# New cost figures in a planned kernel, the memory transposed by the host, the filters' network first, a bias read backwards

## The chip, the cores and the metric

The kernel runs on one core of a Trainium2 chip. The metric is device time in microseconds (us), the median over runs. Engines are named as in the profile: PE (TensorE, the matrix products; PEld its weight loads), DVE (VectorE), ACT (ScalarE), POOL (GpSimd), SP (SyncE, which issues nearly all DMAs).

## The reference, cut to what matters

Two layers act on 256 tokens of width 1024, with a second input `mem` of 256 rows.

- Layer 0: `h = rmsnorm(x)`; `z = h @ hy_w_in` (1024 x 2048). Three of its four blocks of 512 channels go through a short convolution and a gated long convolution (Hyena, order 2). The long filters come from a small network: `h = sin(fr * (feats @ w1 + b1))`, `h = sin(fr * (h @ w2 + b2))`, `h @ w3`, times a decay, divided by the sum of magnitudes, then a transform. The fourth block is the query of a cross attention over `m = rmsnorm(mem)`, with `kv = m @ w_kv`. Both halves go through `w_out`, then a SwiGLU feed-forward with hidden width 2816.
- Layer 1: `z = h @ at_w_in` (1024 x 5120): dilated attention with 3 groups x 4 heads of width 128 and a bias from a table of relative positions, `s = q k / sqrt(128) + bias`, softmax, and the groups combined; again cross attention over `mem`, `w_out`; then a mixture of 8 experts, of which each token takes 2: `(silu(x @ wg[e]) * (x @ wu[e])) @ wd[e]`.

All in float32. The weights of the eight experts alone are 277 MB.

## The kernel before, in words

**Arithmetic.** A float32 factor is split in two parts of type float32r, `hi` (ACT, a rounding copy) and `lo` (DVE, the rest): `split`. A product is three matmuls, hi·hi, hi·lo, lo·hi (`mm3`). Weights come from memory in units of 1 MB (128 x 2048 floats, `load`, kind "stream"); each unit becomes two pairs of 128 x 1024 by one CAST on ACT and one subtraction on DVE each (`weights`, kind "split"), and feeds 12 matmuls of 512 columns (or 24 of 256). Small products of the filters' network are plain float32; each appears in the profile as two MATMUL records. Transposes go through PE with the identity `kt[:, :128]` (`tr`).

**Planner.** Nothing is issued as it is written. Every call (`nc.vector...`, `nc.tensor...`) is recorded by `Plan.add` with a modelled length from `Plan.cost`. `order` then simulates the five queues: `backwards` gives each operation a time by which it has to run (`late`), and going forward each engine takes, of what is ready and finds room, the one with the smallest `late`. Buffers (24 slots of 128 x 2048 floats, 8 PSUM banks) are given out in that simulated order. The result is one fixed order for each engine; on the chip semaphores alone decide the times. A modelled load is bytes / 360e3 us one after the other, and SP does not run more than `BACKLOG` = 6 us ahead of it; a matmul of n float32r columns is max(0.107, 0.0025 + n x 0.4167e-3) us. Kind "dense" marks the weight products, which keep their written order; kind "first" gives an operation a base time 50 us early.

**Stages.** Layer 0's start (`run`, `layer0_mix`): constants `kt`, `sm`; `x` and its norm (`norm_T`), 16 transposes and splits to `hT`; the filters' network (`taps`: product, a chain of vector operations to bring the argument into the range of Sin, Sin, twice), `filters`, `spectrum`; then `memory(0, True)`: `mem` is loaded by rows, squares are summed for its norm (`self.mr`, used later as a scale of the keys), and its rows are transposed (`rows_T`, 16 transposes) and split with the gain to `mT`; first dense block `kv`. Then the Hyena blocks, cross attention, feed-forward, `memory(1, True)` (again loads and transposes `mem`), layer 1, the experts (`moe_layer`, `expert`: per expert 33 units, 396 matmuls of 512 columns), each ending with an indirect DMA that adds its rows to the output (`add_rows`).

**Bias.** `bias_of` reads the bias of a head as a sliding window from a scratch in DRAM, which gives the rows in reversed order. `head` splits it and adds it on PE: two matmuls of 512 columns with the exchange matrix `flip` begin each of the 8 accumulations of scores (4 heads, 2 halves), and softmax reads the scores from PSUM.

Of the kernel before, what the change touches and what calls it, by code (L numbers as in the profile page):

```python
# [13 lines left out]
F32R = mybir.dt.float32r  # L14
# [3 lines left out]
OP = mybir.AluOpType  # L18
# [4 lines left out]
S = 256  # L23
# [5 lines left out]
NB = 32  # L29
NUNIT = 33  # L30


# [3 lines left out]
C_GX, C_GM, C_GK = 58, 82, 90  # L36
N_SM = 106


K_ID, K_FLIP, K_TRI, K_ONE, K_IOTA, K_I8, K_FOLD, K_ROW = 0, 128, 256, 384, 512, 640, 648, 656  # L40
N_K = 660

# [77 lines left out]
class _Eng:  # L120
# [3 lines left out]
    def __getattr__(self, fn):  # L124
# [4 lines left out]
       ("scalar", "vector"): 0.13, ("vector", "scalar"): 0.17, ("scalar", "tensor"): 0.27, ("vector", "tensor"): 0.25}  # L129
FREE = 0.2  # L130
TABLES = {AF.Exp, AF.Silu, AF.Sin}
LOAD = 1.3
# [3 lines left out]
class Plan:  # L136
# [17 lines left out]
    def reset(self):  # L154
        self.ops, self.pe_time = [], 0.0
        for m in self.fixed:
            m.left, m.log, m.end = 0, [], 0.0
        taken = [m.where.i for m in self.fixed if m.kind == "sb"]
        self.whole = [i for i in range(N_SLOT) if i not in taken][::-1]
        self.free = {(dt, k): [] for dt in (F32, F32R) for k in (512, 1024)}  # L160
        self.free_tiny = list(range(N_TINY))[::-1]
        self.free_bank = list(range(8))[::-1]
# [156 lines left out]
    def cost(self, eng, fn, a, kw, aps):  # L319

        n = max((self.width(x) for x in aps), default=1)
        if fn == "add_rows":
            return ISSUE
        if fn == "dma_start":
            ap = aps[0]
            return self.width(ap) * ap.ap[0][1] * 4 / 360e3
        if eng == "tensor":
            if fn == "transpose":
                return 0.109
            r = kw["rhs"]  # L330
            n = self.width(r.on(r.t.ref))
            if kw["rhs_dt"] == F32R:
                return max(0.107, 0.0025 + n * 0.4167e-3)
            return 4 * max(0.054, 0.0025 + n * 0.4167e-3)
        if eng == "scalar":
            ptr = isinstance(kw.get("scale"), View) + isinstance(kw.get("bias"), View)
            return 0.05 + 0.834e-3 * n + 0.2 * ("accum_out" in kw) + 0.09 * ptr
        if eng == "vector":
            return 0.07 + (6.4e-3 if fn == "reciprocal" else 1.04e-3) * n + 0.06 * (fn == "scalar_tensor_tensor")
        if kw.get("op") == OP.pow:  # L340
            return 0.35 + 0.16 * n
        return 0.05 + 2.3e-3 * n if fn == "tensor_tensor" else 0.05 + 3.5e-3 * n if fn == "tensor_copy" else 0.05

    def add(self, eng, fn, a, kw):
        kind, after = kw.pop("kind", None), kw.pop("after", ())
        op = Op()
# [6 lines left out]
        for v in every:  # L353
            w = any(v is o for o in outs)
            lo, hi, p0, p1, ap = self.region(v)
# [8 lines left out]
            for e in m.log:  # L364
                l, h, q0, q1, ew, j = e
# [7 lines left out]
        if fn == "matmul":  # L373
            r = kw["rhs"]
# [20 lines left out]
    def order(self):  # L395
# [35 lines left out]
        while done < len(ops):  # L431
# [9 lines left out]
            while queue and queue[0].start is not None:  # L441
                queue.pop(0)
            self.frontier = queue[0].late
            while self.coming and self.coming[0][2].base is not None:
# [75 lines left out]
    def backwards(self):  # L520
# [45 lines left out]
        for op in ops:  # L566
            op.late = op.rev

# [50 lines left out]
class _Kernel:  # L619
# [229 lines left out]
    def run(self):  # L849
# [16 lines left out]
        self.ident = kt[:, K_ID:K_ID + 128]  # L866
        self.flip = plan.at([128, 128], "flip", F32R)
        nc.scalar.copy(out=self.flip, in_=kt[:, K_FLIP:K_FLIP + 128])
        self.tri = kt[:, K_TRI:K_TRI + 128]
# [8 lines left out]

        nc.scalar.activation(self.tiny(8), self.mhalf, AF.Sin, kind="first")
        xt = plan.x  # L880
        self.x = [xt[:, a * D:(a + 1) * D] for a in range(2)]
# [177 lines left out]
    def layer0_mix(self):  # L1059
        nc, io = self.nc, self.io  # L1060
        hT, dft = self.pair(2048), self.pair(512)
        h8 = hT.rearrange("p (k t) -> p k t", k=8)
        by_parity = lambda t: t.rearrange("p (k t) -> p k t", k=2)
        self.norm_T(self.x, self.scaled(hT, C_GX, natural=True))
        taps = self.taps()
        w3 = self.load(io["w3"], 1024)
# [7 lines left out]
        self.filters(*taps, w3, decay, skip, by_parity(raw))  # L1074
        kT = self.memory(0, True)

# [45 lines left out]
    def memory(self, l, keys):  # L1122

        if keys:
            rows = self.tokens(self.io["mem"])
            if not l:
                self.mr = [self.rms(t) for t in rows]
            self.mT = self.pair(2048)
            self.rows_T(rows, self.scaled(self.mT, C_GK + 8 * l))
        ps = self.dense_block(self.lhs(self.mT))  # L1130
        t = self.pair(1024)
        (self.heads_T if keys else self.rows_of)(ps, t, rms=self.mr)
        return t
# [91 lines left out]
    def head(self, h, at, vecs, out):  # L1225

        nc = self.nc
        hk = self.pair(1024)
        self.split(hk, self.bias_of(vecs, h))
        hk = hk.rearrange("p (a n) -> p a n", a=2)  # L1230
        q, k, v = ([at[f"{n}{g}", h] for g in range(3)] for n in "qkv")
        half = lambda p, a: p[:, a * 128:(a + 1) * 128]
        pT = self.pair(1024).rearrange("p (s a t) -> p s a t", s=4, a=2)
        for a in range(2):
            ps = self.bank()
            nc.tensor.matmul(ps, lhsT=self.flip, rhs=hk.hi[:, a], start=True, stop=False)
            nc.tensor.matmul(ps, lhsT=self.flip, rhs=hk.lo[:, a], start=False, stop=False)
            self.mm3(ps[:, :256], half(q[0], a), k[0], False, False)
            for g in (1, 2):
                self.mm3(ps[:, 128 + 128 * g:256 + 128 * g], half(q[g], a), half(k[g], a), False, g == 2)  # L1240
            sc = self.slot(512)
            g1 = lambda t: t.rearrange("p (z k) -> p z k", z=1)
            self.softmax_rows(g1(ps), 1, g1(sc))
            tp = self.bank()
            for s in range(4):
                self.tr(tp[:, s * 128:(s + 1) * 128], sc[:, s * 128:(s + 1) * 128])
            self.split(pT[:, :, a], tp.rearrange("p (s t) -> p s t", s=4))
        po = self.bank()
        for s in range(2):
            self.mm3(po[:, :256], half(v[0], s), pT[:, s].rearrange("p a t -> p (a t)"), s == 0, False)  # L1250
        for s in (2, 3):
            for a in range(2):
                self.mm3(po[:, a * 128:(a + 1) * 128], half(v[s - 1], a), pT[:, s, a], False, s == 3 and a == 1)
        self.split(out[:, h], po[:, :256])
# [248 lines left out]
def _constants():  # L1503
    c = {}
    k = np.zeros((128, N_K), np.float32)
    k[:, K_ID:K_ID + 128] = np.eye(128)
    k[:, K_FLIP:K_FLIP + 128] = np.eye(128)[::-1]
    k[:, K_TRI:K_TRI + 128] = np.triu(np.ones((128, 128)), 1)
# [27 lines left out]
    oh = np.zeros((33, 5, 256), np.float32)  # L1536
    r = np.arange(255) - 127
    for kind in range(5):
# [41 lines left out]
def _inputs(v):  # L1580
# [21 lines left out]
    io["x"] = v["x"][0]  # L1602
    io["mem"] = v["mem"][0]
    io["rel_bias"] = v["rel_bias"]
    fw = np.zeros((64, 448), np.float32)
# [28 lines left out]
```

## Time and profile before

| what | value |
|---|---|
| median of 3 runs | 1332.57 us (1332.44 to 1333.93) |
| profiled execution, its own time | 1331.97 us |
| its span, first to last instruction | 1330.1 us |
| PE busy / DVE busy / ACT busy | 1307.0 / 1077.9 / 895.7 us |
| memory moved | 372.84 MB, mean 280 GB/s |
| mean granted clock of TensorE | 0.998 |

PE's matmuls overlap: the length of one record (397 ns for 512 columns) is longer than the step from one to the next, so a row "x85, 19.55 us" has 84 steps and one length. Nearly all instructions are issued by one line of the planner (L299), so groups are told apart by their tiles: `b` is a PSUM bank, `s` a slot, `tiny` a small buffer, `kt` the constants.

### The profile page before, as it was taken

To read this page: it belongs to the slowest core of one execution; us is meant where nothing else is said; L and a number is where in the kernel's file an instruction comes from. 1 tells how busy PE (TensorE), PEld (TensorE's weight loads), DVE (VectorE), ACT (ScalarE), POOL (GpSimd) and SP (SyncE) were. 2 spreads that over 40 slices of the span, in tenths; PEclk is the share of its full clock that TensorE was granted. 3 is DMA by queue.
4 is the path that set the end of the run, shared out by engine and by line. 5 is a ranking of instruction groups with operands and counts; after the bars stand their busy time and mean duration, and the time that the engine had idled before them with its cause. 6 is when DMAs were issued, how large, how long until landed. Compare 5 with 4: busy or idle time off the path is not lost.

```text
span 1330.1 us, 16843 instructions
## 1 busy us (share of the span) xinstructions
PE 1307.0 (98%) x6256; PEld 1073.6 (81%) x6256; DVE 1077.9 (81%) x1429; ACT 895.7 (67%) x1190; POOL 41.3 (3%) x38
## 2 busy tenths in 40 slices
PE   6999999999999999999999999999999999999997
PEld 4798888888878888888888888888888778777775
DVE  7989775554578777898999989999988888988886
ACT  7455754444566566687877777876876777777774
POOL 0100000000001000000000000000000000000000
PEclk9999999999999999999999999999999999999999
DMA  9548533357435456299999999999999999999992
GB/s 370 222 146 293 212 138 129 134 187 271 173 127 207 126 172 248 97 371 354 341 375 348 342 367 356 356 375 360 336 365 368 364 351 345 376 360 351 368 354 77
DMA packets 57437, 372.84 MB, mean 280 GB/s; under 512 B 6415, under 2 KB 10595, under 8 KB 13700
## 3 DMA queue, kind: packets, MB, share of 16 engines
q1 hardware_dynamic: 56196, 367.49, 73.8%
q0 software_dynamic: 1152, 4.19, 1.7%
q8 instruction: 51, 0.84, 0.2%
q14 instruction: 38, 0.31, 0.1%
HBM read 365.88 MB, written 5.79 MB: 279 GB/s over the span
## 4 chain that ended last, share of the span: by engine, by line
PE 88%; issue 7%; ACT 2%; DMA 1%; DVE 1%; SPq 0%; POOL 0%; POOLq 0%; ACTq 0%; DVEq 0%
PE b L299 88%; ACT s L299 2%; DVE s L299 1%; DMA out<-s,tiny 1%; DMA sm<-sm 0%; SPq L299 0%; POOL out L296 0%; POOLq L1375 0%; DVE tiny L299 0%; ACTq L299 0%; DVE cg L299 0%; POOLq L296 0%; DVEq L299 0%
## 5 line engine op out<-in xcount | busy, mean ns | idle before, releaser
L299 PE MATMUL b<-s,s 128*128 128x512 f32 (+1 forms) x5674 | 1279.0, 383 | 2.9 <-DVE s L299 0.9
L299 PEld LDWEIGHTS b<-s,s 128*128 128x128 f32 x5674 | 1003.9, 188 | 215.3 <-DVE s L299 15.0
L299 DVE TENSOR_TENSOR s<-s,s 128x1024 fp32r<-128x1024 f32 (+3 forms) x729 | 832.7, 1187 | 124.5 <-ACT s L299 123.6
L299 ACT CAST s<-s 128x1024 fp32r<-128x1024 f32 (+1 forms) x705 | 689.8, 1039 | 128.6 <-PE b L299 96.6
L299 DVE TENSOR_TENSOR s<-b,s 128x512 f32<-128x512 f32 (+5 forms) x206 | 123.0, 609 | 63.4 <-ACT s L299 58.9
L299 ACT CAST s<-b 128x512 fp32r<-128x512 f32 (+3 forms) x118 | 58.3, 504 | 130.5 <-PE b L299 127.4
L299 ACT ACTIVATE s<-b 128x512 f32<-128x512 f32 (+3 forms) x81 | 42.9, 539 | 68.7 <-PE b L299 68.6
L299 PE MATMUL b<-kt,s 128*128 128x128 f32 (+1 forms) x480 | 88.1, 273 | 1.2 <-DVE s L299 1.0
L299 PEld LDWEIGHTS b<-kt,s 128*128 128x128 f32 x480 | 65.1, 146 | 18.6 <-ACT s L299 2.2
L299 ACT ACTIVATE s<-b,tiny 128x512 f32<-128x512 f32 (+2 forms) x58 | 34.0, 611 | 28.0 <-PE b L299 20.7
L299 DVE SCALAR_TENSOR_TENSOR s<-b,sm,s 128x256 fp32r<-128x256 f32 (+1 forms) x88 | 38.0, 478 | 8.2 <-ACT s L299 6.6
L299 ACT ACTIVATE s<-b,sm 128x256 fp32r<-128x256 f32 (+1 forms) x84 | 35.2, 487 | 11.9 <-PE b L299 11.4
L296 POOL DMA_INDIRECT out<-s,tiny x8 | 14.4, 1794 | 761.3 <-ACT s L299 569.5
L299 POOL TENSOR_TENSOR tiny<-tiny,mhalf 128x1 f32<-128x1 f32 (+4 forms) x23 | 26.5, 1152 | 341.5 <-DVE tiny L299 327.1
L299 ACT ACTIVATE s<-x 128x512 f32<-128x512 f32 x16 | 10.1, 631 | 17.7 <-DVE x L299 13.5
L299 PE MATMUL b<-s 128*128 128x512 f32 (+4 forms) x40 | 11.9, 389 | 10.0 <-DMA s<-fw 5.9
L299 DVE TENSOR_TENSOR tiny<-tiny 128x1 f32<-128x1 f32 (+4 forms) x81 | 12.2, 156 | 10.2 <-ACT s L299 8.3
L299 DVE TENSOR_REDUCE tiny<-b 128x2 f32<-128x512 f32 (+3 forms) x25 | 12.3, 495 | 9.5 <-PE b L299 9.4
L299 DVE TENSOR_REDUCE tiny<-s 128x4 f32<-128x512 f32 (+3 forms) x26 | 13.9, 558 | 5.3 <-ACT s L299 5.3
L299 PEld LDWEIGHTS b<-s 128*128 128x128 f32 (+2 forms) x40 | 6.7, 195 | 11.6 <-DMA s<-fw 5.9
L299 DVE TENSOR_TENSOR x<-b,x 128x512 f32<-128x512 f32 x12 | 8.3, 691 | 9.1 <-PE b L299 9.0
L299 ACT COPY s<-b 128x512 f32<-128x512 f32 x11 | 6.3, 584 | 13.6 <-PE b L299 13.4
(65 smaller groups left out, 157.4 us busy)
## 6 DMA issues: line engine op xcount, KB each, us to landing
s<-w_moe SPq DMA_DIRECT2D x264, 1024.0 KB, 7.1
s<-w_ffn SPq DMA_DIRECT2D x33, 1024.0 KB, 4.9
s<-w_at SPq DMA_DIRECT2D x20, 1024.0 KB, 5.1
s<-w_kv SPq DMA_DIRECT2D x8, 1024.0 KB, 7.9
s<-w_hy SPq DMA_DIRECT2D x8, 1024.0 KB, 16.3
s<-w_out SPq DMA_DIRECT2D x8, 1024.0 KB, 4.9
s<-mem SPq DMA_DIRECT2D x4, 512.0 KB
out<-x SPq DMA_DIRECT2D x3, 512.0 KB
```

The lines of the kernel that those rows point to most:

```text
L296: self.nc.gpsimd.indirect_dma_start(out=out, out_offset=bass.IndirectOffsetOnAxis(ap=index, axis=0), in_=rows, in_offset=None, compute_op= ...
L299: getattr(getattr(self.nc, op.eng), op.fn)(*args, **kw)
```

## The change

1. Planner: loads at 390e3 instead of 360e3 bytes per us; float32r matmuls at max(0.11, 0.0137 + n x 0.4167e-3).
2. 14 products of zeros (128 x 128, float32) at the very start, kind "warm", which get `late` = -60; kind "first" for all of `taps()`, which is now called before anything else of the layer.
3. `mem` is also passed in transposed by the host (`mem_t`); `mT` is split from it directly. Layer 0 still loads `mem` by rows for its norm, layer 1 doesn't. `memory(0, True)` is called before the norm of `x`.
4. The table of the bias is written in reverse order; DVE adds the bias to the scores, reading it with a step of -1, into a slot; softmax reads that slot. `flip` and its 16 matmuls, and the split of the bias, are gone.

```diff
+WARM = 14
+RATE = 390e3
-            return self.width(ap) * ap.ap[0][1] * 4 / 360e3
+            return self.width(ap) * ap.ap[0][1] * 4 / RATE
-                return max(0.107, 0.0025 + n * 0.4167e-3)
+                return max(0.11, 0.0137 + n * 0.4167e-3)
-        kind, after = kw.pop("kind", None), kw.pop("after", ())
+        kind, after = kw.pop("kind", self.kind), kw.pop("after", ())
-            self.frontier = queue[0].late
+            self.frontier = max(0.0, queue[0].late)
-            op.late = op.rev
+            op.late = op.rev if op.kind != "warm" else -60.0
...
-        self.flip = plan.at([128, 128], "flip", F32R)
-        nc.scalar.copy(out=self.flip, in_=kt[:, K_FLIP:K_FLIP + 128])
+        idle, ps = self.slot(128), self.bank()
+        nc.vector.memset(idle, 0.0, kind="first")
+        for _ in range(WARM):
+            nc.tensor.matmul(ps[:, :128], lhsT=idle, rhs=idle, start=True, stop=True, kind="warm")
...
+        self.plan.kind = "first"
+        taps = self.taps()
+        self.plan.kind = None
+        kT = self.memory(0, True)
         hT, dft = self.pair(2048), self.pair(512)
         self.norm_T(self.x, self.scaled(hT, C_GX, natural=True))
-        taps = self.taps()
...
         self.filters(*taps, w3, decay, skip, by_parity(raw))
-        kT = self.memory(0, True)
...
         if keys:
-            rows = self.tokens(self.io["mem"])
+            self.mT = self.pair(2048)
+            for h in range(2):
+                raw = self.load(self.io["mem_t"][h], 1024)
+                for k in range(4):
+                    at = (4 * h + k) * S
+                    self.split(self.mT[:, at:at + S], raw[:, k * S:(k + 1) * S],
+                               scale=self.sm[:, C_GK + 8 * l + 4 * h + k:C_GK + 8 * l + 4 * h + k + 1])
             if not l:
-                self.mr = [self.rms(t) for t in rows]
-            self.mT = self.pair(2048)
-            self.rows_T(rows, self.scaled(self.mT, C_GK + 8 * l))
+                self.mr = [self.rms(t) for t in self.tokens(self.io["mem"])]
...
-        hk = self.pair(1024)
-        self.split(hk, self.bias_of(vecs, h))
-        hk = hk.rearrange("p (a n) -> p a n", a=2)
+        bias = self.bias_of(vecs, h).rearrange("p (a s t) -> p a s t", a=2, s=4)
...
             ps = self.bank()
-            nc.tensor.matmul(ps, lhsT=self.flip, rhs=hk.hi[:, a], start=True, stop=False)
-            nc.tensor.matmul(ps, lhsT=self.flip, rhs=hk.lo[:, a], start=False, stop=False)
-            self.mm3(ps[:, :256], half(q[0], a), k[0], False, False)
+            self.mm3(ps[:, :256], half(q[0], a), k[0], True, True)
             for g in (1, 2):
-                self.mm3(ps[:, 128 + 128 * g:256 + 128 * g], half(q[g], a), half(k[g], a), False, g == 2)
+                self.mm3(ps[:, 128 + 128 * g:256 + 128 * g], half(q[g], a), half(k[g], a), True, True)
             sc = self.slot(512)
+            nc.vector.tensor_tensor(out=sc.rearrange("p (s t) -> p s t", s=4), in0=ps.rearrange("p (s t) -> p s t", s=4),
+                                    in1=bias[:, a, :, ::-1], op=OP.add)
-            self.softmax_rows(g1(ps), 1, g1(sc))
+            self.softmax_rows(g1(sc), 1, g1(sc))
...
-    r = np.arange(255) - 127
+    r = 127 - np.arange(255)
```

## Rows read from the trace of the kernel before

**Rows 1.** The page: busy time by engine, share of the span, instructions.

```profile
PE 1307.0 (98%) x6256; PEld 1073.6 (81%) x6256; DVE 1077.9 (81%) x1429; ACT 895.7 (67%) x1190; POOL 41.3 (3%) x38
```

**Rows 2.** Windows, two stretches of the experts: busy per engine, clock, DMA share, GB/s.

```profile
656.81:1029.62 372.81, 372.81 (x1721) 309.30 (x1720) 335.40 (x348) 284.12 (x331) 8.17 (x4) 1.00 0.95 358
1029.62:1322.17 292.55, 289.37 (x1286) 229.58 (x1284) 252.29 (x252) 211.82 (x246) 4.63 (x3) 1.00 0.89 335
```

**Rows 3.** PE's forms in the two stretches: count | busy us, mean ns | idle before.

```profile
L299 PE MATMUL b<-s,s 128*128 128x512 f32 x1561 | 365.7, 392 | 0.0
L299 PE MATMUL b<-kt,s 128*128 128x128 f32 x88 | 15.1, 272 | 0.0
L299 PE MATMUL b<-s,s 128*128 128x256 f32 x64 | 10.0, 282 | 0.0
...
L299 PE MATMUL b<-s,s 128*128 128x512 f32 x1184 | 285.8, 396 | 2.1 <-DVE s L299 0.7
L299 PE MATMUL b<-kt,s 128*128 128x128 f32 x66 | 12.7, 271 | 0.0
L299 PE MATMUL b<-s,s 128*128 128x256 f32 x32 | 5.7, 286 | 0.0
```

**Rows 4.** Timeline of PE alone (start, length): feed-forward, late experts.

```profile
213.74 19.55 PE L299 MATMUL b<-s,s 128*128 128x512 f32 x85
1057.95 14.81 PE L299 MATMUL b<-s,s 128*128 128x512 f32 x61
```

**Rows 5.** Chain that ended last, one late stall: start, length, what.

```profile
1058.71 1.06 ACT s L299
1059.80 1.24 DVE s L299
1061.08 14.64 PE b L299 x64
```

**Rows 6.** Timeline of ACT, one early and one late cast of transposed activations.

```profile
639.30 0.59 ACT L299 CAST s<-b 128x512 fp32r<-128x512 f32 x1 [0.36 <-PE b L299]
1058.23 0.59 ACT L299 CAST s<-b 128x512 fp32r<-128x512 f32 x1 [3.63 <-PE b L299]
```

**Rows 7.** Windows: DMA in the feed-forward and in the start.

```profile
200.00:300.00 100.00, 100.00 (x458) 82.47 (x457) 53.55 (x54) 45.72 (x53) 0.00 (x0) 1.00 0.44 152
10.00:15.00 5.00, 3.90 (x17) 3.25 (x18) 4.11 (x21) 4.37 (x6) 0.59 (x1) 1.00 1.04 421
```

**Rows 8.** The bias: its matmuls, the DVE form it gets, PE in the last head.

```profile
L299 PE MATMUL b<-s,flip x16: 390/393/480, 431.9 to 517.5; 128*128 128x512 f32 x16
L299 DVE TENSOR_TENSOR s<-b,s 128x512 f32<-128x512 f32 x74 | 49.2, 684 | 5.1 <-PE b L299 3.1 <-ACT s L299 2.0
525.36 9.02 PE L299 MATMUL b<-s,s 128*128 128x512 f32 x47
```

**Rows 9.** Timeline of PE: transposes at the start, later 256 columns and transposes.

```profile
12.25 2.39 PE L299 MATMUL b<-kt,s 128*128 128x128 f32 x10
55.77 1.96 PE L299 MATMUL b<-s,s 128*128 128x256 f32 x15
57.57 1.03 PE L299 MATMUL b<-kt,s 128*128 128x128 f32 x8
```

**Rows 10.** The start: the chain's DMA and PE pieces, then PE's first products.

```profile
2.42 5.62 DMA sm<-sm
20.72 37.02 PE b L299 x194
5.86 1.11 PE L299 MATMUL b<-s 33*64 33x256 f32 x2 [5.86 <-DMA s<-fw]
15.39 2.84 PE L299 MATMUL b<-s,s 128*128 128x512 f32 x6
```

**Rows 11.** The end: last products, last indirect DMA.

```profile
1315.54 5.52 PE L299 MATMUL b<-s,s 128*128 128x512 f32 x22
1322.17 1.54 POOL L296 DMA_INDIRECT out<-s,tiny  x1 [95.12 <-ACTq L1376]
```

More of the change, by code (lines that the diff above doesn't have):

```diff
@@ L37 @@
 N_SM = 106
-K_ID, K_FLIP, K_TRI, K_ONE, K_IOTA, K_I8, K_FOLD, K_ROW = 0, 128, 256, 384, 512, 640, 648, 656
-N_K = 660
+K_ID, K_TRI, K_ONE, K_IOTA, K_I8, K_FOLD, K_ROW = 0, 128, 256, 384, 512, 520, 528
+N_K = 532
 N_ROW = S + 128
@@ L154, in reset @@
     def reset(self):
-        self.ops, self.pe_time = [], 0.0
+        self.ops, self.pe_time, self.kind = [], 0.0, None
         for m in self.fixed:
@@ L1506, in _constants @@
     k[:, K_ID:K_ID + 128] = np.eye(128)
-    k[:, K_FLIP:K_FLIP + 128] = np.eye(128)[::-1]
     k[:, K_TRI:K_TRI + 128] = np.triu(np.ones((128, 128)), 1)
@@ L1603, in _inputs @@
     io["mem"] = v["mem"][0]
+    io["mem_t"] = v["mem"][0].reshape(128, 2, 2, 4, 128).transpose(2, 4, 3, 1, 0).reshape(2, 128, 1024)
     io["rel_bias"] = v["rel_bias"]
```

## The prediction

> **What bounds the kernel now.** I read the page first: PE is busy for 1307.0 us of the 1330.1, the other engines for 1077.9 or less [rows 1]. A busy PE is not a PE at its peak, so the next question is how far apart its products start. Windows with the forms inside them answer that. In one stretch of the experts 1561 products of 512 columns, 88 transposes and 64 products of 256 take 372.81 us [rows 2, 3]. A transpose takes (1.03 - 0.27) / 7 = 0.109 us and a product of 256 columns (1.96 - 0.28) / 14 = 0.120 [rows 3, 9]. That leaves (372.81 - 9.6 - 7.7) / 1561 = 0.228 us for a product of 512. The feed-forward gives (19.55 - 0.39) / 84 = 0.228 as well [rows 4], though its DMA is busy for only 0.44 of the time [rows 7]. So 0.228 is the product's own step, and PE is the bound.
>
> One stage is worse. With the same steps the late experts need 1184 x 0.228 + 66 x 0.109 + 32 x 0.120 = 281.0 us, and take 292.55 [rows 2, 3]: 11.6 us lost. Some 1.1 us of it lie after the last product, between 1321.06 and 1322.17 [rows 11]; 10.5 us are stalls. The reader sees them in one row: 61 products at (14.81 - 0.39) / 60 = 0.240 [rows 4]. The chain tells why: a cast of weights on ACT, the subtraction on DVE, then PE [rows 5]. That cast came late because the cast of the transposed activations stood ahead of it in ACT's queue, and ACT sat idle for 3.63 us until PE had made those transposes; early on the same place costs 0.36 us [rows 6]. It is an order that the planner wrote, not a lack of engine time.
>
> The rest of the loss is the start: PE runs without a break only from 20.72 us [rows 10].
>
> All sums stand against the profiled execution: 1331.97 us, span 1330.1, 1.9 us around it. The median shown is 1332.57, 0.6 more, which I add at the end.
>
> **1. The planner's lengths: -10.5 us.** A unit is 12 products and, from rows 3, (88 x 0.109 + 64 x 0.120) / (1561 / 12) = 0.13 us of other work on PE. In the plan of before a unit's products took 12 x (0.0025 + 512 x 0.0004167) = 2.59, with the rest 2.72 us, and its load 1.0486 MB / 360e3 = 2.91. The plan believed the loads to be slower, by 0.19 us a unit. Whatever it had loaded ahead was used up by that: after about 150 units (429 us from 571 to 1000, at 2.86) it had lost 28 us, ten loads, an estimate that fits 24 slots less those of the other buffers. From there the plan waits for each load, and interleaves its casts as if PE had time. The bad order begins at the place where this sum puts it. In the new plan a unit is 12 x 0.2271 + 0.13 = 2.86 on PE and 2.69 for the load: loads keep ahead to the end, and the order of the early experts should go on. I take all 10.5 us. Ends: nothing gained (the order stays), and on the other side the late order over the whole stage, priced under the rivals. That all orders change with the lengths costs or gains elsewhere what I can't compute; I count it at zero, between -2 and +2, since PE's step in the feed-forward leaves nothing to gain [rows 4].
>
> The Trainium skill, "TensorE: Matmul & The Clock Gate", section "Part 2: What happens when you issue a matmul", gives columns / 2.4 + 2.5 ns for the step of back-to-back products, 0.216 us for 512. By it the old length was right and the new one is 5% too long; 396 products an expert would then make each expert 4.5 us shorter on chip than in the new plan. This trace does not agree: 0.228 in two stages.
>
> **2. The bias without flip: -3.6 us.** 16 products [rows 8] at 0.228 leave PE, in a stage where it has no gaps. ACT loses a cast of 1024 per head, DVE a subtraction of 1024, and DVE gets two additions of 512 at 0.684 [rows 8]. Such an addition stands between scores and maximum, 0.7 us in each chain. While blocks of weights follow, those cover it. For the last head the cover is the first half of `w_out`: 47 products in a row from 525.36 on [rows 8]; without it the 0.7 us would be paid once or twice. The step of -1 stands in no row; the nearest is the plain addition, and I take its 0.684; the ends are 0 and twice that, 8 x 0.7 = 5.5 us of DVE time, nearly all beside PE. Ends of the step: -3.6 and -2.2.
>
> **3. Transposes of `mem`: -2.6 us.** 32 of them at 0.109 [rows 9]. The 16 of layer 1 lie between weight products and count in full, 1.75. Of the 16 of layer 0 eight run before 20.72 us, where PE is not the bound, eight after: 0.87. ACT and DVE split the same columns as before. Ends: -3.5 and -1.7.
>
> **4. The start: -2.5 us.** Now the network's first product waits for its load until 5.86 us and the chain on DVE for `sm` until 2.42 + 5.62 = 8.04, because two loads of `x` of 512 KB stand around them in SP's queue [rows 10]. With "first" the two small loads lead. What then holds the first product back is the warming: 14 products, two passes each. At the first transposes a pass takes (2.39 - 0.47) / 9 = 0.213 us, half speed, that is 1.2 GHz; later 0.109, 2.4 GHz [rows 9]; the 0.47 is an estimate of the length of one at half speed. So 28 passes take between 3.1 and 6.0 us and end between 4 and 7 us: the first product comes at about 6, as now, but its chain goes on at once instead of at 8.14. That brings the filters' products (15.39, [rows 10]) forward by some 1.6 us. The 16 transposes of `x` run at full speed: 1.0 us less. Against that, 1.05 MB of `mem_t` come on top in a queue that is full (421 GB/s, [rows 7]): 2.5 us, mostly beside the work of ACT and DVE, which fills 4.4 and 4.1 of the 5 us from 10 us on [rows 7]. I take -2.5 us, near the sum of the two shifts. Ends: -6 (PE takes up the `kv` products in the gap before 20.72) and +4 (2.5 us of loads and a late first product).
>
> **Sum.** -10.5 - 3.6 - 2.6 - 2.5 = -19.2: 1331.97 - 19.2 = 1312.8, and 0.6 for the median: 1313.4. I say 1313 us. With the ends of 2 to 4 and the 2 us of reordering its own range is 1308 to 1322.
>
> **Rivals.**
> A. *The experts are held by supply, not by the plan.* DMA is busy for 0.95 of the early stretch at 358 GB/s [rows 2], a unit every 2.93 us; then a better order gains nothing in step 1. Only 2 to 4 remain: 1332.6 - 8.7 = 1323.9. For it: that 0.95. Against it: the same queue moved 421 GB/s at the start [rows 7], and the stall's chain ends in ACT and DVE, not in a load [rows 5]. Chance 0.12. The skill's rule on steps of 0.216 would speak for this rival: then 0.228 is a product waiting for something; the feed-forward speaks against that.
>
> B. *The start gets worse.* `late` = -60 puts the warming in front of everything on PE, and the extra loads delay `w_hy`: +4 instead of -2.5. 1319.9. For it: ACT, DVE and DMA are nearly full from 10 us on [rows 7]. Against: the one load in the chain of the start is that of `sm` [rows 10]. Chance 0.11.
>
> C. *The new plan is too trusting, and the kernel slower.* If units land later than each 2.69 us, ACT's queue holds casts of units that have not landed ahead of those that PE needs; the late pattern then spreads over the stage from 571 us on. Its price is 10.5 / 292.55 = 0.036 us per us; over the 429 us before 1000 that is +15.4, and step 1 gains nothing: 1332.6 - 8.7 + 15.4 = 1339.3. It outweighs steps 2 to 4 once it has taken 8.7 / 0.036 = 240 us more of the stage. For it: 358 GB/s is below 390. Against: 358 is what PE asks for (2.86 a unit is 367 GB/s), and a plan that trusted loads 8% less had the good order where it had loads in hand. Chance 0.06.
>
> D. *The warming and "first" change nothing*, since ACT and DVE bound the start: step 4 is 0, 1315.9, inside the forecast's own range.
>
> **How the numbers follow.** The forecast with D has 0.71; A 0.12, B 0.11, C 0.06. The range of 8 in 10 leaves out C and the far parts of the others: 1305 to 1325; the low end allows step 4's -6 and 2 us of better order more. A difference under 0.2% (2.7 us) can't be told from none. Forecast, A and B are faster by more than that (0.94, less 0.02 for A with B together); C is slower, less a little where it stops halfway: faster 0.92, same 0.03, slower 0.05.
>
> **What would show it.** Step 1: in the late experts 61 products in a row take 14.1 instead of 14.8 us, ACT no longer sits 3.6 us before the cast of transposed activations, and the last three experts take 282 us or less between their indirect DMAs instead of 292.55. Step 2: no row with `flip`, 8 more additions of 512 on DVE, no new gap of PE near 525 us. Step 3: 32 fewer transposes, still 0.228 around them. Step 4: transposes at 0.109 from the first, the filters' first product of 512 columns near 13.7 instead of 15.39. The prediction is wrong if the late order stays (then 1322 or more), or if PE waits for loads in the experts.

## The result

The changed kernel takes 1317.05 us (1316.08 to 1317.54), against 1333.05 us for the kernel before in the runs beside it: a ratio of 0.9879 (0.9861 to 0.9896). The forecast was 1313 us, in a range of 1305 to 1325. The profiled execution took 1316.60 us, its span is 1314.7; before it was 1331.97. So 15.4 us are gone, where the sum forecast 19.2.

To see where, I cut each execution at instructions that every version has: the last DVE addition of layer 0's mix to `x`, the last one of its feed-forward, the first and the last of layer 1's mix, and the last indirect DMA. "Late" is the time between the starts of the last 1184 products of 512 columns, so that the same products are compared whatever stands between them.

| us | layer 0 | feed-forward | layer 1 | experts | late | median |
|---|---|---|---|---|---|---|
| before | 156.84 | 199.62 | 177.95 | 780.73 | 291.30 | 1333.05 |
| after | 153.69 | 198.19 | 176.06 | 772.21 | 281.23 | 1317.05 |
| difference | -3.15 | -1.43 | -1.89 | -8.52 | -10.07 | -16.0 |

The first and last addition of layer 1 lie 7.03 and 6.80 us apart, and behind the last indirect DMA the span loses 0.2: -3.15 - 1.43 - 1.89 - 0.23 - 8.52 - 0.2 = -15.4.

**Profile after.** The page's busy times: PE has 20 instructions less, and 9 us less.

```profile
PE 1298.1 (99%) x6236; PEld 1073.8 (82%) x6236; DVE 1082.4 (82%) x1434; ACT 903.9 (69%) x1185; POOL 42.0 (3%) x38
```

Windows of the changed kernel, columns as in [rows 2]: the stretch between its first and fifth indirect DMA, that from there to the last, the feed-forward and the start.

```profile
650.16:1029.94 379.78, 379.78 (x1746) 313.56 (x1746) 344.59 (x354) 296.92 (x337) 6.59 (x4) 1.00 0.96 372
1029.94:1306.95 277.01, 276.01 (x1263) 227.43 (x1261) 248.03 (x250) 214.11 (x241) 4.77 (x4) 1.00 0.84 328
200.00:300.00 100.00, 100.00 (x462) 82.41 (x461) 53.64 (x54) 45.45 (x55) 0.00 (x0) 1.00 0.45 161
10.00:15.00 5.00, 2.94 (x7) 1.77 (x7) 4.76 (x12) 5.00 (x11) 0.09 (x1) 0.61 1.00 370
```

The late stretch holds fewer products than in [rows 2, 3], since the indirect DMAs stand elsewhere in the order; the two lengths must not be set against each other. PE's forms in it give the step. (277.01 - 1.0 - 66 x 0.109 - 32 x 0.120) / 1161 = 0.228 us for a product of 512 columns; 1.0 us is the end after the last product, 1305.95 to 1306.95, as in [rows 11].

```profile
L301 PE MATMUL b<-s,s 128*128 128x512 f32 x1161 | 271.8, 392 | 0.0
L301 PE MATMUL b<-kt,s 128*128 128x128 f32 x66 | 11.2, 271 | 0.0
L301 PE MATMUL b<-s,s 128*128 128x256 f32 x32 | 5.2, 281 | 0.0
```

The end in the timeline (PE's last products, the last indirect DMA):

```profile
1301.35 4.60 PE L301 MATMUL b<-s,s 128*128 128x512 f32 x19
...
1306.95 1.54 POOL L298 DMA_INDIRECT out<-s,tiny  x1 [85.05 <-ACT s L301]
```

The same steps in the timeline of PE: 61 products in (14.21 - 0.39) / 60 = 0.230 us each on average, where [rows 4] had 0.240. These are averages: the median step from one product of 512 columns to the next is 0.227 us in both kernels, and the stalls are single long steps. Among the last 1184 products, 90 steps are above 0.240 us in the kernel before and 24 in the changed one.

```profile
1054.38 18.91 PE L301 MATMUL b<-s,s 128*128 128x512 f32 x82
1073.48 14.21 PE L301 MATMUL b<-s,s 128*128 128x512 f32 x61
```

ACT was idle for 3.63 us before the cast of transposed activations in [rows 6]; before the two there now it is idle for 0.99 us and not at all:

```profile
1042.82 0.59 ACT L301 CAST s<-b 128x512 fp32r<-128x512 f32 x1 [0.99 <-PE b L301]
1056.03 0.58 ACT L301 CAST s<-b 128x512 fp32r<-128x512 f32 x1
```

The chain that ended last (start, length, what) passed at the same time through ACT, DVE and PE in turn [rows 5]. Now it is PE alone from 509.81 to 1177.90 us; behind that the view follows ACT, DVE and the queue of the indirect DMAs, and no longer tells of PE:

```profile
357.44 147.49 PE b L301 x770
...
509.81 668.09 PE b L301 x3109
```

DVE's additions of the bias are in one group with the plain ones of [rows 8], 8 more than before at the same mean, and those of the last head take 0.65 each; reading with a step of -1 costs nothing that shows:

```profile
L301 DVE TENSOR_TENSOR s<-b,s 128x512 f32<-128x512 f32 x82 | 54.3, 683 | 5.8 <-PE b L301 4.0 <-ACT s L301 1.7
487.07 1.29 DVE L301 TENSOR_TENSOR s<-b,s 128x512 f32<-128x512 f32 x2 [1.21 <-PE b L301]
```

The start on PE (start, length, idle before): the warming with the network's first product, its second, and then the weight products of `kv`, which the filters' products [rows 10] now follow.
```profile
1.06 5.47 PE L301 MATMUL b<-s 128*128 128x128 f32 x30 [1.06 <-DVE s L301]
9.46 0.70 PE L301 MATMUL b<-s,s 64*128 64x256 f32 x2 [2.94 <-ACT s L301]
10.81 1.88 PE L301 MATMUL b<-s,s 128*128 128x512 f32 x4 [0.65 <-ACT s L301]
14.10 2.50 PE L301 MATMUL b<-s,s 128*128 128x512 f32 x5 [1.41 <-DVE s L301]
```

In the windows of the start the granted clock falls from 1.00 to 0.50, that is from 2.4 to 1.2 GHz, and comes back.

```profile
8.00:12.00 4.00, 1.89 (x5) 1.26 (x6) 3.83 (x7) 3.01 (x7) 0.00 (x0) 0.88 0.99 403
12.00:16.00 4.00, 2.59 (x7) 1.52 (x6) 3.86 (x11) 4.00 (x8) 0.09 (x1) 0.50 0.99 343
16.00:20.00 4.00, 4.00 (x15) 3.23 (x14) 3.87 (x12) 4.00 (x15) 0.31 (x1) 0.76 1.01 418
```

Two places are worse. Layer 1 has waits of PE that were not there, at its first transposes (PEld and PE, for ACT) and near 508 us (for DVE, in the chain of the cross attention):

```profile
357.44 0.44 PE L301 MATMUL b<-kt,s 128*128 128x128 f32 x2 [0.39 <-ACT s L301]
508.58 0.51 PE L301 MATMUL b<-s,s 128*128 128x256 f32 x2 [0.56 <-DVE s L301]
```

### The profile page after: what moved, and what is told of

Read it like the earlier page. It is cut to its first block, busy times and chain, and to the rows that moved or that the text cites. A ratio compares the mean times of both kernels' runs of the same rounds, so it can differ in the third digit from the quotient of the medians.

```text
span 1314.7 us, 16854 instructions
## 1 busy us (share of the span) xinstructions
PE 1298.1 (99%) x6236; PEld 1073.8 (82%) x6236; DVE 1082.4 (82%) x1434; ACT 903.9 (69%) x1185; POOL 42.0 (3%) x38
## 4 chain that ended last, share of the span: by engine, by line
PE 88%; issue 7%; DVE 3%; ACT 1%; DMA 1%; POOL 0%; POOLq 0%; ACTq 0%; DVEq 0%
PE b L301 88%; DVE s L301 3%; ACT s L301 1%; DMA out<-s,tiny 1%; DVE tiny L301 0%; POOL tiny L301 0%; POOL out L298 0%; DVE x L301 0%; POOLq L1387 0%; ACTq L301 0%; POOLq L298 0%; DVEq L301 0%
## 5 line engine op out<-in xcount | busy, mean ns | idle before, releaser
L301 PE MATMUL b<-s,s 128*128 128x512 f32 (+2 forms) x5678 | 1270.0, 382 | 6.4 <-ACT s L301 3.6
L301 PEld LDWEIGHTS b<-s,s 128*128 128x128 f32 (+1 forms) x5678 | 1009.0, 188 | 212.3 <-DVE s L301 6.7
L301 DVE TENSOR_TENSOR s<-s,s 128x1024 fp32r<-128x1024 f32 (+2 forms) x728 | 835.0, 1185 | 140.7 <-ACT s L301 137.9
L301 ACT CAST s<-s 128x1024 fp32r<-128x1024 f32 (+1 forms) x701 | 699.9, 1038 | 244.2 <-PE b L301 124.3
L301 PE MATMUL b<-kt,s 128*128 128x128 f32 (+1 forms) x448 | 78.0, 271 | 0.4 <-ACT s L301 0.4
L301 ACT ACTIVATE s<-b,tiny 128x256 f32<-128x256 f32 (+2 forms) x50 | 28.6, 598 | 12.3 <-PE b L301 11.7
L301 DVE TENSOR_REDUCE tiny<-s 128x4 f32<-128x512 f32 (+4 forms) x34 | 19.3, 586 | 7.7 <-ACT s L301 7.5
L301 ACT ACTIVATE s<-s,tiny 128x256 f32<-128x256 f32 (+1 forms) x32 | 18.4, 616 | 7.6 <-DVE tiny L301 7.6
L301 ACT ACTIVATE s<-x 128x512 f32<-128x512 f32 x16 | 10.1, 629 | 10.5 <-DVE x L301 9.8
L301 PE MATMUL b<-s 128*128 128x128 f32 (+3 forms) x64 | 14.5, 349 | 1.1 <-DVE s L301 1.1
L301 DVE TENSOR_TENSOR s<-b,tiny 128x512 f32<-128x512 f32 (+3 forms) x26 | 13.7, 559 | 0.6 <-PE b L301 0.4
```

The lines of the kernel that those rows point to most:

```text
L301: getattr(getattr(self.nc, op.eng), op.fn)(*args, **kw)
```

## The experiments

All are compared with the kernel before, run beside them on the same chip. Stages in us, columns as above; the ratio is to the kernel before.

| kernel | layer 0 | feed-forward | layer 1 | experts | late | median | ratio |
|---|---|---|---|---|---|---|---|
| e1, before + both lengths | 155.37 | 199.64 | 181.53 | 773.07 | 281.85 | 1325.77 | 0.9944 (0.9930 to 0.9958) |
| e7, before + length of loads | 156.53 | 199.66 | 177.96 | 771.18 | 280.77 | 1322.25 | 0.9917 (0.9904 to 0.9931) |
| e8, before + length of products | 155.58 | 200.05 | 180.21 | 772.54 | 281.28 | 1326.20 | 0.9947 (0.9934 to 0.9961) |
| e4, before + bias read backwards | 155.18 | 199.61 | 174.80 | 780.88 | 291.42 | 1328.21 | 0.9961 (0.9948 to 0.9975) |
| e5, before + transposed memory | 157.07 | 198.30 | 177.83 | 780.95 | 291.46 | 1330.74 | 0.9982 (0.9973 to 0.9991) |
| e13, before + network first | 155.05 | 199.66 | 177.83 | 780.89 | 291.40 | 1330.67 | 0.9987 (0.9978 to 0.9996) |
| e2, after with old lengths | 157.38 | 198.28 | 175.71 | 780.97 | 291.50 | 1329.62 | 0.9972 (0.9962 to 0.9983) |
| e14, after, old length of products | 154.39 | 198.28 | 175.68 | 771.29 | 281.09 | 1316.17 | 0.9878 (0.9863 to 0.9893) |
| e3, after, no warming planned | 153.69 | 198.57 | 179.13 | 773.02 | 282.39 | 1320.75 | 0.9903 (0.9888 to 0.9919) |
| e11, after, warming not issued | 154.04 | 198.19 | 176.11 | 772.20 | 281.22 | 1316.18 | 0.9867 (0.9852 to 0.9882) |
| e6, after, 12 more warming products | 157.19 | 198.19 | 176.11 | 772.21 | 281.23 | 1320.06 | 0.9899 (0.9884 to 0.9914) |
| e10, after, longer power on POOL | 156.32 | 198.24 | 175.85 | 771.03 | 281.09 | 1318.73 | 0.9893 (0.9878 to 0.9908) |

**Both lengths alone (e1), and all but them (e2).**

```diff
-            return self.width(ap) * ap.ap[0][1] * 4 / 360e3
+            return self.width(ap) * ap.ap[0][1] * 4 / 390e3
-                return max(0.107, 0.0025 + n * 0.4167e-3)
+                return max(0.11, 0.0137 + n * 0.4167e-3)
```

e2 is the changed kernel with the old figures of this diff.

> The kernel before with the planner's two lengths alone (loads at 390e3, products at 0.0137 + n x 0.4167e-3). Theory (the order of the late experts): 10 us less than before, near 1323 us; the late experts' stalls are gone and the last three indirect DMAs lie 277 to 282 us apart instead of 292.55. Rival (supply holds the experts): no gain, within 2 us of before. Rival (a new plan shifts stalls elsewhere): the late stalls go, but the whole gains less than 7 us, and the loss shows ahead of the experts.

> The changed kernel with the old lengths (360e3, 0.0025 + n x 0.4167e-3); all else is as changed. Theory: it loses what the late experts gained, 8 to 11 us: 1325 to 1328 us, with stalls of PE after about 1000 us as before the change. Rival (supply): no difference from the changed kernel, 1317.

The late products follow the lengths: 281.85 with them, 291.50 without, whatever the rest of the kernel is. In e2 the rows of before are back, 61 products at (14.83 - 0.39) / 60 = 0.241 and ACT idle for 3.64 us (timelines of PE and ACT of e2):

```profile
1054.98 14.83 PE L301 MATMUL b<-s,s 128*128 128x512 f32 x61
...
1055.26 0.59 ACT L301 CAST s<-b 128x512 fp32r<-128x512 f32 x1 [3.64 <-PE b L301]
```

But e1 gains only 7.5 us in all: its layer 1 is 3.6 us longer. And in the changed kernel the lengths are worth 1329.62 - 1317.05 = 12.6 us, since layer 0 too comes out 3.7 us shorter with them: in e2 PE waits 3.25 us for ACT near 34 us, and the granted clock falls behind it (timeline of PE and windows of e2). One term of the sum has two prices, by what else is in the plan.

```profile
33.89 1.21 PE L301 MATMUL b<-kt,s 128*128 128x128 f32 x8 [3.25 <-ACT s L301]
...
35.00:40.00 5.00, 5.00 (x32) 5.00 (x32) 4.65 (x9) 4.48 (x10) 0.00 (x0) 0.66 1.02 416
```

**Each length by itself (e7, e8; e14 in the changed kernel).** e7 has the first pair of lines of the diff above, e8 the second; e14 is the changed kernel with the old line for products.

> The kernel before with loads at 390e3 alone: a unit is then 2.72 us of modelled work on PE and 2.69 of load. Theory (the plan of before ran out of loads after about 150 units): the late stalls are gone, last residual to last indirect DMA 772 to 774 us instead of 780.7. Rival (both lengths are needed): 777 or more.

> The kernel before with the corrected product length alone: a unit is then 2.86 us of modelled work on PE and 2.91 of load, 0.05 short, 13 us over 264 units, which is less than the ten loads in hand. Theory: the late stalls are gone as well, or begin only in the last expert; last residual to last indirect DMA 772 to 775 us. Rival (any shortfall brings the late order): stalls after about 1000 us, 777 or more.

> The changed kernel with the old length of a product (0.216 us for 512 columns) and the new one for loads. Theory: the length of loads alone gives the good order of the late experts, as it did in the kernel before: the experts take 771 to 773 us, and the time is that of the changed kernel give or take what the other stages' new order does, 1314 to 1320. Rival (with the rest of the change both lengths are needed): late stalls come back, the experts take 776 us or more, and the time is 1321 or more.

Either length removes the late stalls, as the prediction's account has it: a unit's modelled work on PE, less its modelled load, is +0.03 us in e7 and -0.05 in e8, where it was -0.19 in the old plan. So only the sign and size of this difference matter for the order, not that each length is right: e14 with the wrong 0.216 us is as fast as the changed kernel.

The traces show the loads in hand as well. Set the k-th load of the experts' weights against its first cast on ACT, and take the mean time from the issue of the load to that cast, by the time of the cast:

| us | 640 to 720 | 800 to 880 | 960 to 1040 | 1120 to 1200 |
|---|---|---|---|---|
| before | 31.0 | 23.2 | 17.7 | 19.2 |
| e8 | 31.9 | 29.7 | 27.9 | 26.9 |
| e7 | 35.5 | 34.1 | 36.2 | 37.4 |
| after | 33.1 | 33.8 | 35.7 | 37.7 |

In the kernel before the lead shrinks until about 1000 us, where the long steps of PE begin, and then stays near its lowest. In e8 it shrinks slowly and lasts to the end; in e7 and in the changed kernel it does not shrink.

The product's length is also what upsets layer 1 (e8 180.21, e7 177.96). Timelines of e8 for POOL and PE there: PE waits for DVE behind a power on POOL that took 2.70 us.

```profile
378.55 2.70 POOL L299 TENSOR_TENSOR tiny<-tiny,mhalf 128x8 f32<-128x8 f32 x1 [18.47 <-DVE tiny L299]
...
382.57 1.23 PE L299 MATMUL b<-s,s 33*4 33x256 f32 x3 [0.89 <-DVE s L299]
```

In the kernel before, the same power took 1.65 us (timeline of POOL):

```profile
378.79 1.65 POOL L299 TENSOR_TENSOR tiny<-tiny,mhalf 128x8 f32<-128x8 f32 x1 [18.01 <-DVE tiny L299]
```

In e1 the gap is there too, and the granted clock falls behind it, to a mean of 0.80 over 5 us (windows of e1):

```profile
380.00:385.00 5.00, 3.84 (x15) 1.85 (x13) 4.30 (x10) 2.17 (x3) 0.60 (x1) 0.80 0.09 38
```

**A longer power in the plan (e10).**

```diff
-            return 0.35 + 0.16 * n
+            return 1.4 + 0.16 * n
```

> The changed kernel, with the planner's length of GpSimd's power raised from 0.35 + 0.16 n to 1.4 + 0.16 n (2.7 us for 8 columns, the longest that traces showed, instead of 1.6). Theory: the waits of PE behind that power in layer 1 (two, 1.3 us together, in the changed kernel; 3.4 us with the clock at half speed in the kernels with the lengths alone) come from its modelled length; PE then has other work there, and the kernel is 0.5 to 1.5 us faster than the changed one: 1315.5 to 1316.5. Rival: the wait is an accident of each order; the new order has as many such places, and the time lies anywhere from 1314 to 1321 with the waits elsewhere. The experts stay within 1 us of 772 in both.

Behind the power at 375.58 us, which takes 2.70 us here, PE does not wait (timeline of POOL), while e1, e3 and e8 have 0.88 to 0.89 us of idle PE behind one as long. But in the changed kernel that power took 1.65 us and nothing waited for it either, so this place says nothing of the gain. The wait that the changed kernel has at the start of layer 1 (0.39 us at 357.44) is shorter here, 0.25 us at 360.21; the one near 508 us is down to 0.04.

```profile
375.58 2.70 POOL L301 TENSOR_TENSOR tiny<-tiny,mhalf 128x8 f32<-128x8 f32 x1 [16.90 <-DVE tiny L301]
```

The gain is 0.2 us in layer 1 and 1.2 in the experts, of which the additions of layer 1's mix, 1.0 us further apart, take most; layer 0's new order is 2.6 us longer, and the median is 1.7 us higher, in intervals that overlap. The time is the rival's, not the theory's.

**The bias read backwards alone (e4).** The edit is the whole of point 4 of the change; its core:

```diff
...
-            nc.tensor.matmul(ps, lhsT=self.flip, rhs=hk.hi[:, a], start=True, stop=False)
-            nc.tensor.matmul(ps, lhsT=self.flip, rhs=hk.lo[:, a], start=False, stop=False)
+            nc.vector.tensor_tensor(out=sc.rearrange("p (s t) -> p s t", s=4), in0=ps.rearrange("p (s t) -> p s t", s=4),
+                                    in1=bias[:, a, :, ::-1], op=OP.add)
...
```

> The kernel before with the bias read backwards and added on DVE, no flip; nothing else. Theory of the prediction: 3.6 us less (16 products of 0.228), near 1329.5. Rival (the longer chain from scores to softmax makes PE wait in the heads): 1 to 2 us less only, with a wait of PE on DVE or ACT in the stage of the heads, as at 507.75 us in the changed kernel.

Layer 1 is 3.15 us shorter, where 16 x 0.228 = 3.65 of work are gone. The median falls by more, 5.1 us, because layer 0, which the edit hardly touches, also lost 1.66: in the kernel before PE waits 1.82 us in layer 0 after 34 us, most of it in the two places below (timeline of PE); in e4 other products stand there, and it waits for nothing.

```profile
60.23 0.82 PE L299 MATMUL b<-kt,s 128*128 128x128 f32 x4 [0.96 <-DVE s L299]
...
103.40 2.82 PE L299 MATMUL b<-s,s 128*128 128x512 f32 x11 [0.67 <-ACT s L299]
```

**The transposed memory alone (e5).** The edit is that of `memory` in the diff above.

> The kernel before with nothing but the transposed memory. Step 3 as predicted: the feed-forward stage (with layer 1's memory in it) 1.4 us shorter, 198.2 instead of 199.6, as in the changed kernel; in all 2.6 us less than before, 1330.7. Rival (every new plan moves layers 0 and 1 by chance, as the lengths alone moved layer 1 by +3.5 us): the feed-forward is still 1.4 us shorter, but the first part of layer 0 and layer 1 move by up to 3 us either way, 1328 to 1334. The experts stay at 780 to 781 us in both, since the lengths are the old ones.

The feed-forward stage is 1.32 us shorter, as expected. Layer 0 gains nothing (157.07): PE waits there 2.29 us in all after 34 us, against 1.82 before, and behind the waits near 60 us the granted clock falls (timeline of PE and windows of e5).

```profile
60.83 1.22 PE L299 MATMUL b<-s 128*128 128x512 f32 x2 [0.56 <-ACT s L299]
...
60.00:65.00 5.00, 4.44 (x14) 3.50 (x14) 4.45 (x7) 2.15 (x4) 0.00 (x0) 0.66 0.08 13
```

PE has 32 transposes less; in groups of four they cost less than 0.109 each, since a product starts 0.35 us after the first of four (1040.57 to 1040.92 us in the timeline of the changed kernel): 16 x 0.088 = 1.4.

**The network first alone (e13).**

```diff
...
+        self.plan.kind = "first"
+        taps = self.taps()
+        self.plan.kind = None
+        kT = self.memory(0, True)
...
-        taps = self.taps()
...
-        kT = self.memory(0, True)
```

> The kernel before with nothing but the filters' network and the memory first: no warming, no transposed memory, old lengths, flip kept. Step 4 as predicted: the last residual of layer 0's mix comes 2.5 us earlier than 156.84, and so does the end: about 1330.8. Rival one, the warming does the work of the start: then nothing is gained here, 157 and 1333. Rival two, the transposes of the memory now stand at the very start and wait for its rows, so the start is longer: 158 to 160 and 1335 or more.

Layer 0 is 1.79 us shorter without any warming. The network's first product leaves at 3.53 instead of 5.86 us, its second at 7.58 instead of 11.10 (timeline of PE of e13); what comes next waits for the constants, and from 30 to 33 us PE waits 1.97 us more. Up to 34 us PE idles 10.7 us in all, against 10.2 before, so the earlier chain does not show as less idle time at the start; after 34 us it idles for nothing, against 1.82 us before.

```profile
3.53 1.11 PE L299 MATMUL b<-s 33*64 33x256 f32 x2 [3.53 <-DMA s<-fw]
7.58 1.22 PE L299 MATMUL b<-s,s 64*128 64x256 f32 x2 [2.94 <-ACT s L299]
11.02 2.79 PE L299 MATMUL b<-kt,s 128*128 128x128 f32 x12 [2.22 <-DMA kt<-consts]
...
32.03 0.63 PE L299 MATMUL b<-s,s 128*128 128x256 f32 x3 [1.36 <-DVE s L299]
```

**The warming: not planned (e3), planned but not issued (e11), almost doubled (e6).** e11 and e6 keep the changed kernel's orders on every engine, so only the warming differs. In e6 the 12 added products stand behind the network's first product.

```diff
# e3
-        idle, ps = self.slot(128), self.bank()
-        nc.vector.memset(idle, 0.0, kind="first")
-        for _ in range(WARM):
-            nc.tensor.matmul(ps[:, :128], lhsT=idle, rhs=idle, start=True, stop=True, kind="warm")
# e11
+                if op.kind != "warm":
                     self.emit(op, ...)
# e6
+                if op.kind == "warm":
+                    again = op
+                elif op.eng == "tensor" and again is not None:
+                    for _ in range(12):
+                        self.emit(again, ...)
+                    again = None
```

> The changed kernel without the 14 warming products. In the changed kernel's trace the clock rises at 4.24 us, falls at 11.06 and rises again at 17.89, and 12 of the first weight products run at half speed. Theory (the warming is given back): within 1 us of the changed kernel. Rival (the warming is worth the step's 1.0 us and the two network products): 1 to 2.5 us slower. Rival (the warming holds the first network product back): up to 1 us faster, the first product starting below 5.9 us.

> The changed kernel's own orders on every engine, with the 14 warming products planned but not issued. The run without them in the plan too was 3.7 us slower, with the same times at the end of layer 0 (146.9 and 153.7 us) and a wait of PE at 378 us in layer 1. Theory (on the chip the warming is given back, the 3.7 us are the new order): within 0.7 us of the changed kernel, 1316.5 to 1318. Rival (the products themselves are worth it): 1320 to 1321.

> The changed kernel's own orders, with 12 more warming products right behind the network's first product, so that PE stays at work from 6.5 to about 9.3 us. Theory A (the clock then stays up and the first weight products run at 0.228, but PE waits for ACT and DVE at 24.9 to 32 us anyway): the 12 products at half speed are gone, and the end of layer 0 moves by less than 0.7 us. Theory B (the half speed is what the start still loses): 1.5 to 2.5 us faster, the end of layer 0 as much earlier.

Without it (timelines of PE and DVE of e11) the network's first product starts at 3.44 us instead of 5.88, DVE's chain at 4.59 instead of 6.56, and the long run of `kv` at 13.57 instead of 14.10 (its first four products stand in the row of 8.41, behind the network's second), but at half speed: with 0.63 us for the length of one record, (4.63 - 0.63) / 9 = 0.44 us a product.

```profile
3.44 1.11 PE L301 MATMUL b<-s 33*64 33x256 f32 x2 [3.44 <-DMA s<-fw]
8.41 3.42 PE L301 MATMUL b<-s,s 64*128 64x256 f32 x6 [3.87 <-ACT s L301]
13.57 4.63 PE L301 MATMUL b<-s,s 128*128 128x512 f32 x10 [1.74 <-DVE s L301]
...
4.59 0.54 DVE L301 TENSOR_SCALAR s<-b,sm 64x256 f32<-64x256 f32 x1 [0.55 <-PE b L301]
```

In the changed kernel the first products of that run are no better, (2.50 - 0.63) / 4 = 0.47: PE idles for 2.94 us before the network's second product, and the clock the warming had raised is at 0.50 by 12 us. What it gives (products step at 0.23 us from 18.0 us on, against 19.3) and what it takes (2.4 us on the chain) cancel: layer 0 153.69 against 154.04, medians 1317.05 against 1316.18, with ratios whose intervals overlap. e3 is 3.7 us slower than the changed kernel with layer 0 the same to 0.01 us: a new order in layer 1 (179.13) with the gap of e1, not the missing warmth. In e6 DVE waits for the first product until the added ones are through (timelines of PE and DVE of e6), and layer 0 ends 3.5 us later:

```profile
1.06 8.59 PE L301 MATMUL b<-s 128*128 128x128 f32 x54 [1.06 <-DVE s L301]
12.59 0.70 PE L301 MATMUL b<-s,s 64*128 64x256 f32 x2 [2.94 <-ACT s L301]
...
9.69 0.54 DVE L301 TENSOR_SCALAR s<-b,sm 64x256 f32<-64x256 f32 x1 [5.62 <-PE b L301]
```

The clock fell all the same (0.50 from 16 to 20 us), so this run doesn't show what a clock held at 1.00 would be worth.

No version is clearly faster than the changed kernel; e11 and e14 are even with it.

## Why the prediction was right, and where it was off

The time lies in the range, 4 us above the forecast, because the largest term had the right cause and nearly the right size.

**Step 1 (-10.5; measured -8.5 in the experts).** The cause was right: the stalls were a planned order, they begin where loads in hand run out, and e1, e2, e7, e8 and e14 switch them off and on with the lengths. The ten loads in hand were worked back from that place, so the place itself was no test of the sum; what tests it is that e7 and e8 came out as it says, and that the lead of the loads shrinks to its lowest there. In the late products -10.07 of the forecast 10.5 arrived. Two things were missed. The first 2012 products of 512 columns in the experts' stage became 1.45 us longer (the middle 1561 from 373.38 to 374.33 us, the first 451 from 113.09 to 113.59); no row shows a stall, it is 0.7 ns a product, its cause is open, and e1, e7 and e8 have 1.1 to 1.7 of it as well. And the effect of new orders elsewhere was counted as 0, between -2 and +2; e1 shows +3.6 in layer 1, and e2 against the changed kernel -3.7 in layer 0. The bound of 2 was too narrow: a bound for "all orders change" needs the range that other orders of the same stage show, here 177.8 to 181.5 us for layer 1 with `flip` and 174.8 to 179.1 without, and the one trace of before doesn't give that.

**Step 2 (-3.6; -3.15 alone, -1.9 in the changed kernel).** The work went, 3.65 us, and the reversed read costs nothing that shows. Layer 1 does not keep all of it: measured from start to start of the products, the changed kernel loses 0.55 us near 357 and 0.97 from 507.75 to 509.81 us, 1.5 together (its rows call 0.39 and 0.60 of them idle), where PE in the kernel before does not wait. The wait near 357 goes with the product's length (e1 and e8 have it, e7 and e14 don't). The prediction looked for a gap near 525, behind the last head's additions; those are done by 488.4, and the wait is in the cross attention's chain behind them. None of the six kernels with `flip` waits there.

**Step 3 (-2.6; -1.4 in the feed-forward).** Layer 1's 16 transposes counted as forecast, a little less each. What those of layer 0 are worth, 0.87 in the forecast, stays open: alone (e5) they bring nothing, but there a half-speed stretch of the clock behind new waits stands against them, and in the changed kernel no run separates them from step 4.

**Step 4 (-2.5; layer 0 -3.15).** The size was about right, but not by the way that was forecast, so part of it is luck. The chain ran as forecast: the first product at 5.88, DVE at 6.56, the second product at 9.46 instead of 11.10, 1.6 us earlier. But the filters' products did not move from 15.39 to 13.7, since `kv` goes first and they follow at 26, and no gain from transposes at full speed shows. What shows is that the waits of 1.82 us after 34 us, shown under e4, are gone. From 40 us to the last addition of layer 0's mix, those waits taken off, there are 156.84 - 40 - 1.82 = 115.0 us in the kernel before, 115.05 in e13 and 113.7 in the changed kernel. So the 1.79 us of e13 are the waits, and its start is no shorter; e4, e1 and e8, in which the network stays where it was, lost these waits too. Of the 3.15 us in the changed kernel 1.82 are the waits; the other 1.33 are near what 16 transposes less are worth (an estimate, 16 x 0.088 = 1.4). Whether the network's place took the waits away, or another new order would have done as well, is not shown: no run puts the network back in the changed kernel. With the old lengths (e2) steps 2 to 4 together leave layer 0 at 157.38. The warming shows no part in the gain: without it layer 0 is 154.04 (e11).

**The rivals.** A, supply: refuted, DMA now moves 372 GB/s in the same stage at 0.96, and the late products run at 0.228. B, a worse start: what it feared of the warming is real (2.4 us on the chain), but is paid back; the 3.5 us of e6's longer warming are not. C, a plan that trusts loads too much: refuted, with the same trust in loads neither the changed kernel nor e7 (771.18) has the late stalls. D, warming and first change nothing: true of the warming (e11), and not refuted for the network's place, since e13's gain lies in waits that e4 lost too.

**Adding up.** Medians of the parts alone: e1 -7.5, e4 -5.1, e5 -2.3, e13 -2.4, together -17.3 against -16.0 measured. That the sum nearly fits hides that its parts are not those forecast: e4 and e13 have 1.7 and 1.8 us from the same waits in layer 0, e1 pays 3.6 in layer 1. The step that fell short is step 1 with its clause on other orders: 2.0 us in the experts; the other 1.7 are step 2's, in layer 1. The sum's own range, 1308 to 1322, is a little narrower than its ends make it: added straight, they give 1307 to 1324.

The Trainium skill's 0.216 us for a back-to-back product ("TensorE: Matmul & The Clock Gate", section "Part 2: What happens when you issue a matmul") stays at odds with the rows: with the stalls gone, the step is 0.228 still.

## What to carry to other kernels

Where a program writes the order, its cost figures matter by their differences: compare the modelled times of the two resources that race (here a unit's products and its load), and see over how many units the difference uses up what is in hand; that told beforehand that either new length would remove the stall. Any edit to such a plan redraws all stages, which here moved layers 0 and 1 by up to 3.7 us from one order to another: judge a part by its own stage, in the same instructions before and after, look which waits came and went there, and don't read 3 us of the total as the worth of an edit. Warming an engine is only worth what the chain behind it doesn't pay.

## Not expected of the hardware

POOL's power of 128x8 values takes 1.65 or 2.55 to 2.70 us for the same operation, in one order or another; in e10 one took 3.62 (474.60 us). What decides it stays open: no run here varied one thing alone. The granted-clock column reads 1.00 in the first 16 us of e11 although its products step at 0.44 us there, half speed, and from 10 to 15 us in the kernel before [rows 7], where transposes step at 0.213 us [rows 9]; so the column isn't to be trusted before the first change that the trace records, and the step between products is the better witness. A gap of PE of about 1 us in layer 1 left the clock at 1.00 in e8, and was followed by half speed for 3.4 us in e1; the runs don't show what tells the two apart.
